# Gate and up projections of two feed-forward layers by one level of Strassen, with moving weights and token-major results

## The chip, the core and the metric

The kernel runs on one core of one Trainium2 chip, as one program. The metric is the device time of one execution in microseconds, taken as the median of several runs. In the profile PE is TensorE (its weight loads, which overlap its matmuls, stand as PEld), DVE is VectorE, ACT is ScalarE, POOL is GpSimd and SP is SyncE, whose queue starts the loads of the weights.

## The reference

Two layers, 512 tokens, 1024 features, 2816 hidden features, all in float32. Layer 0 mixes tokens by a gated linear recurrence (RG-LRU), layer 1 by stick-breaking attention with 16 heads. Each mixer is followed by a feed-forward part, which is what the change touches:

```python
for layer in range(DEPTH):
    h = _rmsnorm(x, norm_mix_g[layer])
    x = x + mixer(h)                        # RG-LRU or attention
    h = _rmsnorm(x, norm_ffn_g[layer])
    g = h @ w_gate                          # 512x1024 @ 1024x2816
    u = h @ w_up                            # 512x1024 @ 1024x2816
    x = x + (silu(g) * u) @ w_down          # 512x2816 @ 2816x1024
return _rmsnorm(x, final_g)
```

`_rmsnorm` multiplies each token by 1/sqrt(mean of its squares + 1e-6) and each feature by g.

## The kernel before

**Layout.** The activations stand transposed: eight tiles `x[0..7]` of 128 features (partitions) x 512 tokens. A product is made in PSUM banks of 128 x 512, with a 128 x 128 block of weights as the stationary operand and activations as the moving one. Each operand is split into a rounded high part (type fp32r) and a remainder, and a product is three matmuls (`mm3`, L163 to L167): high x high, high x low, low x high.

**Weights.** They come in chunks of 128 x 1024 elements (512 KB), in the order of one list made by `plan` (L81). `chunk` (L151) hands out the next one, and on the way starts loads (four chunks ahead, on SP's queue, into four buffers `raw`) and splits (two ahead, three buffers each of `wh` and `wl`): ScalarE casts raw to wh (L136), and VectorE or GpSimd takes wl = raw - wh (L137; `wl_engine` gives odd chunks to GpSimd and even ones to VectorE, but for a few given by hand).

**The norm.** As soon as a tile x[k] has its residual added, `norm_in` (L215) makes its two operands uh and ul (ScalarE L219, VectorE L220) without the token's factor, and `norm_sq` (L229) squares it on ScalarE (L235) and adds the square into `acc` (L237; GpSimd, the last tile on VectorE). `norm_rs1` (L251) sums acc over partitions by four one-column matmuls (L255), and `rsqrt` makes the token factors `rsT`, one token a partition. `norm_rs2` (L259) spreads them over all partitions by four matmuls (L263), into `rsB`.

**A feed-forward layer** (`ffn`, L455) has 22 tiles of 128 hidden features. Each is a gate product and an up product of 24 matmuls (8 feature tiles x 3) and an evacuation (L460 to L468): both are multiplied by rsB on VectorE, the gate goes through Silu on ScalarE, and the product of both is split into `fh` and `fl`. norm_rs1 stands behind the first gate product, norm_rs2 behind the first up product. All 22 pairs stay in SBUF. Then the eight output tiles follow, each 22 x 3 matmuls over three chunks (`DOWN_SPLIT`), and a residual addition (L490). In layer 1 the last output tile is made in two halves of 256 tokens (L493 to L501), so that `finish` (L266), which makes the final norm and writes the output for one half of the tokens, works on the first half while TensorE makes the second.

The last part of each mixer is its output projection: tile by tile 24 matmuls, a residual addition (L450 in layer 0, L731 in layer 1) and `norm_in`. The order on each engine's queue comes from a scheduler that follows data and priorities; the splits of weights have a raised priority (L143). In the attention the order on PE, ACT, DVE and POOL is written out by hand.

Of the kernel before, what the change touches and what calls it, by code (L numbers as in the profile page):

```python
# [16 lines left out]
P = 128  # L17
S = 512
# [11 lines left out]
NSLOT = 73  # L30
WARM = 9
DOWN_SPLIT = ((0, 8), (8, 15), (15, 22))
# [9 lines left out]

class Kern:
    def __init__(self, ctx, tc, a, out):
        self.ctx, self.tc, self.nc, self.a, self.out = ctx, tc, tc.nc, a, out
        mk = lambda name, bufs, **kw: ctx.enter_context(tc.tile_pool(name=name, bufs=bufs, **kw))
        self.const = mk("const", 1)
        self.wp = mk("wp", 1)
        self.tp = mk("tp", 1)
        self.ar = mk("ar", 1)  # L50
        self.free = deque(range(NSLOT))
        self.slot = {}
        pp = mk("pp", 1, space=bass.MemoryType.PSUM)
        self.bank = [pp.tile([P, S], F32, name=f"bank{i}") for i in range(8)]
        self.bi = 0
        self.tn = 0
        self.wl_dve = False
        self.wl_on = {**dict.fromkeys((*range(5, 12), 14), self.nc.gpsimd),
                      **dict.fromkeys((2, 3, 4, 12, 13, 15, 16, 17, 18, 19), self.nc.vector)}
# [6 lines left out]
    def new(self, name, dt=F32, shape=None):  # L66
        i = self.free.popleft()
        self.tn += 1
        t = self.ar.tile(shape or [P, S], dt, tag=f"s{i}", bufs=1, name=f"{name}_{self.tn}")
        self.slot[id(t)] = (i, t)  # L70
        return t

    def rel(self, *ts_):
        for t in ts_:
            self.free.append(self.slot.pop(id(t))[0])
# [5 lines left out]
    def plan(self):  # L81
# [13 lines left out]
        def ffn(l):  # L95
            r = []
            for f in range(NF):
                r += [a["w_gu"][l, f, 0], a["w_gu"][l, f, 1]]
            for m in range(8):
                r += [a["w_dn"][l, m, :, lo * P:hi * P] for lo, hi in DOWN_SPLIT]  # L100
            return r

        full += ffn(0)
        full += [a["w_v"][c] for c in range(8)]
# [5 lines left out]
        self.wq = {}  # L110
        self.loaded = self.split = self.used = 0
# [4 lines left out]

    def raw_tile(self, i):
        t = self.wp.tile([P, 1024], F32, tag="raw", bufs=4, name=f"raw{i}")
        self.raw[i] = (t, self.chunks[i].shape[-1])
# [3 lines left out]
    def load_one(self):  # L123
        src = self.chunks[self.loaded]
        t = self.raw_tile(self.loaded)
        self.nc.sync.dma_start(t[:, :src.shape[-1]], src)

    def split_tiles(self, i):
        wh = self.wp.tile([P, 1024], F32R, tag="wh", bufs=3, name=f"wh{i}")
        wl = self.wp.tile([P, 1024], F32R, tag="wl", bufs=3, name=f"wl{i}")  # L130
        self.wq[i] = (wh, wl)
        self.split += 1
# [6 lines left out]
    def split_one(self):  # L139
        i = self.split  # L140
        raw, n = self.raw.pop(i)
        wh, wl = self.split_tiles(i)
        with self.tc.high_priority(self.PRI):  # L143
            self.split_piece(i, raw, wh, wl, slice(0, n))

    def wl_engine(self, i):
        if i in self.wl_on:
            return self.wl_on[i]
        return self.nc.gpsimd if i % 2 and not self.wl_dve else self.nc.vector

    def chunk(self, ahead=None):  # L151
        i = self.used
        self.used += 1
        n = len(self.chunks)
        while self.loaded < min(n, i + self.AHEAD_LOAD):
            self.load_one()
        while self.split < min(n, i + (ahead or self.AHEAD_SPLIT)):
            self.split_one()
            while self.loaded < min(n, self.split + self.AHEAD_LOAD - self.AHEAD_SPLIT + 1):
# [18 lines left out]
    def setup(self):  # L178
# [3 lines left out]
        self.u = [None] * KT  # L182
        self.par = c.tile([P, NPAR], F32, name="par")
# [40 lines left out]

    def free_u(self):
# [13 lines left out]
    def rsqrt(self, ss, lo, hi):  # L239
# [8 lines left out]
        for t in range(lo, hi):  # L248
            self.dgi = nc.vector.tensor_scalar(self.dg[:, ts(t)], self.ident, self.rsT[:, t:t + 1], None, ALU.mult)

    def norm_rs1(self):  # L251
# [4 lines left out]
        self.dg = self.tmp()  # L256
# [41 lines left out]
    def rglru(self):  # L298
        nc, tc = self.nc, self.tc
        with ExitStack() as cx:  # L300
            rp = cx.enter_context(tc.tile_pool(name="rg", bufs=1))
# [21 lines left out]
            def evac_x(m, ps):  # L323
                xc[m], ah[m], al[m] = self.new("xc"), self.new("ah", F32R), self.new("al", F32R)
# [63 lines left out]
            def tile_x2():  # L388
                p = (self.ps(), self.ps())
                raws = [self.raw.pop(i)[0] for i in range(2)]  # L390
# [56 lines left out]
            for m in range(KT):  # L447
# [3 lines left out]
                self.norm_in(m, "g_ffn0")  # L451
# [3 lines left out]
    def ffn(self, l, gnext):  # L455
        nc, tc = self.nc, self.tc
        if True:
            ah, al = [None] * NF, [None] * NF

            def evac(f, pg, pu):  # L460
                tg, tu = self.tmp(), self.tmp()
                nc.vector.tensor_tensor(tg, pg, self.rsB, ALU.mult)  # L462
                self.last = nc.scalar.activation(tg, tg, AF.Silu)
                nc.vector.tensor_tensor(tu, pu, self.rsB, ALU.mult)  # L464
                nc.vector.tensor_tensor(tu, tu, tg, ALU.mult)
                ah[f], al[f] = self.new("fh", F32R), self.new("fl", F32R)
                nc.scalar.copy(ah[f], tu)  # L467
                nc.gpsimd.tensor_tensor(al[f], tu, ah[f].bitcast(F32), ALU.subtract)  # L468

            for f in range(NF):  # L470
                pg = self.ps()
                self.mm_tile(pg, self.u)
                if f == 0:
                    self.norm_rs1()
                pu = self.ps()
                self.mm_tile(pu, self.u)
                if f == 0:
                    self.norm_rs2()
                evac(f, pg, pu)
            self.free_u()  # L480
# [3 lines left out]
            for m in range(KT if gnext else KT - 1):  # L484
                p = self.ps()
                for lo, hi in DOWN_SPLIT:
                    wh, wl = self.chunk()
                    for k in range(lo, hi):
                        self.mm3(p, wh[:, ts(k - lo)], wl[:, ts(k - lo)], ah[k], al[k], k == 0, k == NF - 1)
                nc.vector.tensor_tensor(self.x[m], self.x[m], p, ALU.add)  # L490
                self.norm_in(m, gnext)
            if gnext is None:
                ws = [self.chunk() for _ in DOWN_SPLIT]  # L493
                for j in range(2):
                    cs = ts(j, HS)
                    p = self.ps()
                    for (lo, hi), (wh, wl) in zip(DOWN_SPLIT, ws):
                        for k in range(lo, hi):
                            self.mm3(p[:, :HS], wh[:, ts(k - lo)], wl[:, ts(k - lo)], ah[k][:, cs], al[k][:, cs],
                                     k == 0, k == NF - 1)  # L500
                    self.finish(j, p)  # L501
            for t in ah + al:
                self.rel(t)

    def attention(self):
# [4 lines left out]
        with ExitStack() as cx:  # L510
            ap_ = cx.enter_context(tc.tile_pool(name="att", bufs=1))
            vs = [[None] * 4 for _ in range(NT)]
# [24 lines left out]
            for half in range(2):  # L537
# [12 lines left out]
                for t in range(NT):  # L550
                    r = self.rsT[:, t:t + 1]
                    pvv = pv[t].rearrange("p (h d) -> p h d", d=64)
                    for j in range(2):
                        v = vs[t][2 * half + j] = self.new("vs", F32R, [P, 4, P])
# [149 lines left out]
            with tc.manual_schedule(engines={E.PE, E.Activation, E.DVE, E.Pool}):  # L704
# [10 lines left out]
                def osplit(p):  # L715
                    oh, ol = ou[p] = self.new("oh", F32R), self.new("ol", F32R)
# [13 lines left out]
                def out_evac(m):  # L730
                    nc.vector.tensor_tensor(self.x[m], self.x[m], outs.pop(m)[0], ALU.add)  # L731
                    self.norm_in(m, "g_ffn1")
# [74 lines left out]
def layout(inp):  # L807
# [7 lines left out]
    def cols(v):  # L815
# [11 lines left out]
    gu = np.stack([np.stack([stat(g("ffn_w_gate")[l]), stat(g("ffn_w_up")[l])], axis=1) for l in range(2)])  # L827
    dn = np.stack([stat(g("ffn_w_down")[l]) for l in range(2)])
# [9 lines left out]
        "w_gu": c(gu),  # L838
        "w_dn": c(dn),
# [17 lines left out]
```

## Time and profile before

| | |
|---|---|
| time, median of 3 runs | 1214.06 us (1213.08 to 1214.74) |
| time of the profiled execution | 1214.85 us |
| span of the profiled execution | 1213.1 us, 13743 instructions |
| mean granted clock of TensorE | 0.995 |
| data from HBM | 102.81 MB, 86 GB/s over the span |

The span runs from the first to the last instruction of the profiled execution, and the time holds what lies around it too. Of a stretch (A:B), a row gives its length, then for PE, PEld, DVE, ACT and POOL the busy time with the number of instructions, then the mean granted clock (1.00 is full), the share of the time that the DMA engines were busy, and GB/s. A row of a timeline has the start in us, the duration, the engine, the line, the operation, and output <- input. A row of a group has the line, the engine, the operation, the number of instructions, the busy time, the mean duration in ns, and the idle time of the engine ahead of them with what ended it; where a source line is looked at, the three figures are the least, the median and the greatest duration in ns. Buffer numbers are left out of the names.

### The profile page before, as it was taken

The numbers are of one execution on the slowest core, as the hardware profiler recorded it, in microseconds if no ns is written. First come the engines' busy times: TensorE is split into PE (matmuls) and PEld (weight loads), VectorE is DVE, ScalarE is ACT, GpSimd is POOL, SyncE is SP. The second block draws the span as 40 slices with busy tenths as digits, with TensorE's granted clock in tenths as the row PEclk, the third lists the DMA queues.
The fourth block names the chain that finished last, engine by engine and source line by source line (L and its number), as shares of the span: only waits on it lengthen the run. The fifth ranks groups of instructions, "written<-read, shape, count | busy, mean of one in ns | idle before, by whom it ended". The sixth has DMA issues, their size and how long they took to land.

```text
span 1213.1 us, 13743 instructions
## 1 busy us (share of the span) xinstructions
PE 1165.5 (96%) x5347; PEld 955.4 (79%) x5347; DVE 581.4 (48%) x790; ACT 521.6 (43%) x751; POOL 457.8 (38%) x283
## 2 busy tenths in 40 slices
PE   9999999999999999999978888799999999999996
PEld 6877788888888888888857766578888888888886
DVE  7878652333223222223799999975322233321112
ACT  6687443323323222224677777654323232332221
POOL 2442343333333223321266665533333333332332
PEclk9999999999999999999999999999999999999998
DMA  7222322232323333332111111122222223233321
GB/s 241 79 82 92 117 88 89 102 104 87 104 87 100 96 96 96 100 105 87 53 35 35 38 50 36 35 70 95 97 90 101 91 101 105 85 96 96 96 64 70
DMA packets 31313, 105.80 MB, mean 87 GB/s; under 512 B 3600, under 2 KB 4624, under 8 KB 31248
## 3 DMA queue, kind: packets, MB, share of 16 engines
q1 hardware_dynamic: 30960, 104.40, 26.8%
q8 instruction: 42, 0.69, 0.2%
q10 hardware_dynamic: 288, 0.52, 0.1%
q14 instruction: 23, 0.19, 0.0%
HBM read 102.81 MB, written 2.10 MB: 86 GB/s over the span
## 4 chain that ended last, share of the span: by engine, by line
PE 74%; DVE 14%; issue 3%; ACT 1%; POOL 0%; DVEq 0%; ACTq 0%; POOLq 0%
PE bank L165 24%; PE bank L167 24%; PE bank L166 24%; DVE sph L636 2%; DVE t L635 2%; DVE wl L137 2%; DVE r L642 1%; DVE awh L678 1%; DVE awl L683 1%; DVE o L701 1%; DVE ql L590 1%; DVE ks L597 1%; DVE t L576 1%; PE bank L662 1%; DVE t L641 0%
## 5 line engine op out<-in xcount | busy, mean ns | idle before, releaser
L136 ACT CAST wh<-raw 128x1024 fp32r<-128x1024 f32 (+2 forms) x202 | 203.4, 1010 | 531.6 <-PE bank L166 279.0
L165 PE MATMUL bank<-uh,wh 128*128 128x512 f32 x960 | 376.8, 393 | 9.0 <-DVE t L576 8.1
L167 PE MATMUL bank<-uh,wl 128*128 128x512 f32 x960 | 374.0, 390 | 1.3 <-DVE wl L137 1.3
L166 PE MATMUL bank<-ul,wh 128*128 128x512 f32 x960 | 373.8, 389 | 0.3 <-DVE ul L220 0.3
L137 POOL TENSOR_TENSOR wl<-raw,wh 128x1024 fp32r<-128x1024 f32 (+2 forms) x95 | 219.6, 2312 | 361.5 <-ACT wh L136 361.5
L165 PEld LDWEIGHTS bank<-uh,wh 128*128 128x128 f32 x960 | 180.6, 188 | 47.8 <-issue 9.5
L167 PEld LDWEIGHTS bank<-uh,wl 128*128 128x128 f32 x960 | 180.2, 188 | 40.5 <-DVE wl L137 2.5
L166 PEld LDWEIGHTS bank<-ul,wh 128*128 128x128 f32 x960 | 180.4, 188 | 37.2 <-DVE ul L220 0.6
L137 DVE TENSOR_TENSOR wl<-raw,wh 128x1024 fp32r<-128x1024 f32 (+2 forms) x107 | 136.1, 1274 | 137.2 <-ACT wh L136 136.2
L468 POOL TENSOR_TENSOR fl<-t,fh 128x512 fp32r<-128x512 f32 x44 | 67.2, 1528 | 198.4 <-ACT fh L467 198.4
L165 PE MATMUL bank<-fh,wh 128*128 128x512 f32 (+1 forms) x374 | 141.1, 377 | 0.0
L166 PE MATMUL bank<-fl,wh 128*128 128x512 f32 (+1 forms) x374 | 140.8, 376 | 0.0
L167 PE MATMUL bank<-fh,wl 128*128 128x512 f32 (+1 forms) x374 | 140.8, 376 | 0.0
L464 DVE TENSOR_TENSOR t<-bank,rsB 128x512 f32<-128x512 f32 x44 | 30.4, 691 | 199.4 <-PE bank L167 199.4
L462 DVE TENSOR_TENSOR t<-bank,rsB 128x512 f32<-128x512 f32 x44 | 30.4, 691 | 116.7 <-PE bank L167 116.7
L637 POOL TENSOR_TENSOR spl<-t,sph 128x512 fp32r<-128x512 f32 (+1 forms) x48 | 58.8, 1230 | 65.4 <-DVE sph L636 51.6
L166 PEld LDWEIGHTS bank<-fl,wh 128*128 128x128 f32 x374 | 70.4, 188 | 13.0
L167 PEld LDWEIGHTS bank<-fh,wl 128*128 128x128 f32 x374 | 70.4, 188 | 12.9
L165 PEld LDWEIGHTS bank<-fh,wh 128*128 128x128 f32 x374 | 70.4, 188 | 12.7
L237 POOL TENSOR_TENSOR acc<-acc,t 128x512 f32<-128x512 f32 x24 | 38.5, 1606 | 52.1 <-ACT t L235 43.4
L683 POOL TENSOR_TENSOR awl<-t,awh 128x512 fp32r<-128x512 f32 x28 | 40.0, 1427 | 41.2 <-DVE awh L678 41.2
L490 DVE TENSOR_TENSOR x<-x,bank 128x512 f32<-128x512 f32 x15 | 10.3, 687 | 74.7 <-PE bank L167 74.7
(166 smaller groups left out, 1456.4 us busy)
## 6 DMA issues: line engine op xcount, KB each, us to landing
raw<-w_gu SPq DMA_DIRECT2D x88, 512.0 KB, 3.5
raw<-w_dn SPq DMA_DIRECT2D x32, 448.0 KB, 3.3
raw<-w_dn SPq DMA_DIRECT2D x16, 512.0 KB, 3.5
raw<-w_qk SPq DMA_DIRECT2D x16, 512.0 KB, 3.4
raw<-w_in SPq DMA_DIRECT2D x14, 512.0 KB, 3.7
raw<-w_ao SPq DMA_DIRECT2D x8, 512.0 KB, 3.5
raw<-w_v SPq DMA_DIRECT2D x8, 512.0 KB, 3.4
raw<-w_bo SPq DMA_DIRECT2D x8, 512.0 KB, 3.4
```

What stands on the lines that cost most here:

```text
L136: self.nc.scalar.copy(wh[:, c], raw[:, c])
L137: self.wl_engine(i).tensor_tensor(wl[:, c], raw[:, c], wh[:, c].bitcast(F32), ALU.subtract)
L165: mm(out, lhsT=wh, rhs=xh, start=first, stop=False)
L166: mm(out, lhsT=wh, rhs=xl, start=False, stop=False)
L167: mm(out, lhsT=wl, rhs=xh, start=False, stop=last)
L237: self.acci = eng.tensor_tensor(self.acc, self.acc, sq, ALU.add)
L462: nc.vector.tensor_tensor(tg, pg, self.rsB, ALU.mult)
L464: nc.vector.tensor_tensor(tu, pu, self.rsB, ALU.mult)
L468: nc.gpsimd.tensor_tensor(al[f], tu, ah[f].bitcast(F32), ALU.subtract)
L635: nc.vector.scalar_tensor_tensor(sp[:, :w], z, 0.0, e[:, :w], ALU.max, ALU.add)
L637: nc.gpsimd.tensor_tensor(sl[:, :w], sp[:, :w], sh[:, :w].bitcast(F32), ALU.subtract)
L683: eng.tensor_tensor(wl[:, :w], ts_[i][:, :w], hd["wh"][i][:, :w].bitcast(F32), ALU.subtract)
```

## The change

Gate and up of a layer are one matrix product: A (512 tokens x 1024 features) times B (1024 features x gate and up). It is now made by one level of Strassen's method in Winograd's form. A is cut into tokens 0 to 255 and 256 to 511, and into features 0 to 511 and 512 to 1023 (A11, A12, A21, A22). B is cut into quarters b0 (gate, first features), b1 (up, first), b2 (gate, second) and b3 (up, second). In place of eight products of quarters there are seven, in this order:

- 1: A11 with b0
- 5: (A21 + A22) with b1 - b0
- 6: (A21 + A22 - A11) with b3 - b1 + b0
- 3: (A12 - A21 - A22 + A11) with b3
- 7: (A11 - A21) with b3 - b1
- 2: A12 with b2
- 4: A22 with b2 - (b3 - b1 + b0)

The sums of results give gate and up of all 512 tokens.

**Units.** The hidden features are taken in five units of 512 and one of 256 (`Unit`, `FB`, `NU`). A product of a full unit takes two chunks of weights and 4 feature tiles x 2 token tiles x 3 = 24 matmuls, 12 a chunk. The activations are now the stationary operand (128 x 128) and the weights the moving one (512 columns, 256 in the last unit), and the result has tokens on its partitions. So the token factor is a scalar of a partition (rsT), and norm_rs2 is gone in the feed-forward part. Results are gathered in SBUF tiles r1, u2 and b5, two each.

**Operands.** `ffn_in` takes the place of `norm_in` behind the mixers. For tiles 0 to 3 it makes the operand of product 1 alone. For tiles 4 to 7 it scales x[m] and x[m - 4] on ScalarE, makes four sums of 256 tokens on VectorE (L331 and L346), and splits three tiles (ScalarE casts, VectorE remainders). The sums of the weights are made by VectorE too: `Piece.source` (L76) has four for each chunk position, eight a full unit, of 128 x 1024, in place or in two buffers `tt`. All splits of these weights have their remainder on VectorE, those of the down weights on GpSimd.

**The rings.** In the feed-forward part the rings of wh and wl have four buffers, splits run three chunks ahead and loads eight, the latter partly into buffers of the layer's own pool (b1, b3). The arena of 73 slots becomes 43 and a pool of 30 that belongs to the mixers.

**Down, unit by unit.** While unit u is made, the results of unit u - 1 are transposed back by TensorE (`turn`: eight 128 x 128 transposes into two banks, L627; ScalarE copies the high part hh, L630; VectorE subtracts the remainder hl, L631), two of its four tiles behind product 1 and two behind product 5. Four `down_pair` follow between the products, each 24 matmuls (L640 to L642) into the same two banks, and an addition into x (L645). The last unit's turn stands at the end, and behind it eight tiles of six matmuls; in layer 1 the last tile again in two halves with `finish`.

```diff
+    def source(self):
...
+        if q == 7:
+            sub(b(1), b(3), b(1))
...
+        if q == 5:
...
+            sub(b("t"), b(1), b(0))
+        elif q == 6:
+            sub(b("t"), b(3), b("t"))
+        else:
+            sub(b("t"), b(2), b("t"))
+        return b("t")
...
+            def turn(fs, banks):
+                for f, b in zip(fs, banks):
+                    for t in range(NT):
+                        nc.tensor.transpose(b[:, ts(t)], (u2 + b5)[t][:, ts(f)], self.ident)
...
+                    nc.scalar.copy(h, b)
+                    nc.vector.tensor_tensor(lw, b, h.bitcast(F32), ALU.subtract)
...
+                product(1, un, A, 0)
+                for j in range(2):
+                    nc.scalar.copy(r1[j][:, :w], A[j][:, :w])
+                if u == 0:
+                    self.bi = 6
+                    self.norm_rs1(False)
+                else:
+                    turn((0, 1), tb)
+                product(5, un, B, 0)
+                if u > 0:
+                    turn((2, 3), tb)
+                for j in range(2):
+                    nc.scalar.copy(b5[j][:, :w], B[j][:, :w])
+                if u > 0:
+                    down_pair(0)
+                product(6, un, A, 0, False)
...
+                if 0 < u < NU:
+                    down_pair(1)
+                product(3, un, B, 0, False)
...
+            turn((0, 1), (A[0], A[1]))
...
+                    if m == KT - 1 and split7:
+                        for j in range(2):
+                            down(w, i, 2, p7[j], first=False, cs=hs[j])
+                            self.bi = 4 + 2 * j
+                            self.finish(j, p7[j])
+                        continue
```

In the feed-forward part PE's order is written out by hand; the other engines' follows from the scheduler. Three places of the order show what moved.

VectorE at the start of layer 0's feed-forward part. x_7 and x_8 are the last two tiles of x, acc the sum of squares, wl the remainder of a weight chunk, and ul that of an operand. Before:

```order
L450 TENSOR_TENSOR x_7_84<-x_7_84,bank_75 128x512
L220 SCALAR_TENSOR_TENSOR ul_1349<-x_7_84,par,uh_1348 128x512
L450 TENSOR_TENSOR x_8_85<-x_8_85,bank_76 128x512
L137 TENSOR_TENSOR wl_1440<-raw_1321,wh_1439 128x1024
L220 SCALAR_TENSOR_TENSOR ul_1387<-x_8_85,par,uh_1386 128x512
L237 TENSOR_TENSOR acc<-acc,t_1390 128x512
```

Now, from the fourth row behind the addition into x_8 (three sums of 256 tokens stand between): t are operand sums, ol their remainders, tt the sums of weights.

```order
L331 TENSOR_TENSOR ol_1454<-t_1436,oh_1453 128x512
L76 TENSOR_TENSOR tt_1485<-b_178_1473,raw_1244 128x1024
L331 TENSOR_TENSOR t_1438<-t_1436,t_1437 128x256
L76 TENSOR_TENSOR tt_1503<-b_179_1475,raw_1300 128x1024
L234 TENSOR_TENSOR wl_1488<-tt_1485,wh_1487 128x1024
L331 TENSOR_TENSOR ol_1446<-t_1437,oh_1445 128x512
L234 TENSOR_TENSOR wl_1506<-tt_1503,wh_1505 128x1024
L76 TENSOR_TENSOR tt_1485<-b_180_1477,tt_1485 128x1024
L331 TENSOR_TENSOR ol_1450<-t_1438,oh_1449 128x512
L76 TENSOR_TENSOR tt_1503<-b_181_1479,tt_1503 128x1024
L234 TENSOR_TENSOR wl_1535<-tt_1485,wh_1534 128x1024
L371 TENSOR_TENSOR acc<-acc,t_1457 128x512
```

Two rows stood between the last residual addition and that into acc before; now fourteen do, seven of them 1024 wide.

TensorE at the same place. bank_71 is the second bank of product 1, bank_72 the first of product 5. Before (uh and ul are the operands that norm_in made; the rows ahead of L255 end the first gate product):

```order
L165 MATMUL bank_77<-uh_1386,wh_1355 128x512
L166 MATMUL bank_77<-ul_1387,wh_1355 128x512
L167 MATMUL bank_77<-uh_1386,wl_1356 128x512
L255 MATMUL bank_70<-ones,acc 128x1 x4
L165 MATMUL bank_71<-uh_1122,wh_1394 128x512
L166 MATMUL bank_71<-ul_1123,wh_1394 128x512
```

Now:

```order
L621 MATMUL bank_71<-wl_1482,a_130_1234 128x512
L622 MATMUL bank_71<-wh_1481,a_130_1234 128x512
L389 MATMUL bank_76<-ones,acc 128x1 x4
L620 MATMUL bank_72<-wh_1487,oh_1281 128x512
L621 MATMUL bank_72<-wl_1488,oh_1281 128x512
L622 MATMUL bank_72<-wh_1487,ol_1282 128x512
```

The four matmuls that read acc stand 24 matmuls into the layer both times; behind them stood the rest of the layer, and so it does now.

ScalarE at a second turn (unit 1 of layer 0, tiles hh_82 in banks 76 and 77), beside the steady gate and up of before. Before:

```order
L136 CAST wh_1624<-raw_1518 128x1024
L463 ACTIVATE t_1614<-t_1614 128x512
L136 CAST wh_1654<-raw_1558 128x1024
L467 CAST fh_1620<-t_1615 128x512
L136 CAST wh_1694<-raw_1588 128x1024
L463 ACTIVATE t_1684<-t_1684 128x512
```

Now:

```order
L630 CAST hh_80_2677<-bank_76 128x512
L630 CAST hh_80_2685<-bank_77 128x512
L233 CAST wh_2743<-tt_2653 128x1024
L233 CAST wh_2773<-raw_2615 128x1024
L630 CAST hh_82_2728<-bank_76 128x512
L630 CAST hh_82_2736<-bank_77 128x512
L669 COPY b_1471<-bank_72 128x512
L669 COPY b_1472<-bank_73 128x512
```

Two weight casts (L233) stand between the copies of the first turn and those of the second, and the copies of the second stand ahead of the copies of product 5's banks.

357 lines of the change are left out of this document (276 added, 81 removed).

## The prediction

> **What bounds the kernel now.** First the page: its head, the busy shares and the shares of the chain that ended last.
>
> ```profile
> span 1213.1 us, 13743 instructions
> PE 1165.5 (96%) x5347; PEld 955.4 (79%) x5347; DVE 581.4 (48%) x790; ACT 521.6 (43%) x751; POOL 457.8 (38%) x283
> ...
> PE 74%; DVE 14%; issue 3%; ACT 1%; POOL 0%; DVEq 0%; ACTq 0%; POOLq 0%
> ```
>
> TensorE (PE) is busy 96% of the span. A share over a whole kernel hides stages, so next come the busy times by stretches, chosen inside the feed-forward layers (two of layer 0, two of layer 1).
>
> ```profile
> 172.50:345.00 172.50, 172.50 (x771) 143.05 (x770) 52.35 (x73) 55.17 (x68) 61.29 (x31) 1.00 0.29 95
> 345.00:527.50 182.50, 182.50 (x807) 151.12 (x806) 47.52 (x50) 51.23 (x62) 61.38 (x31) 1.00 0.32 96
> 843.50:1021.00 177.50, 177.50 (x793) 147.19 (x792) 54.04 (x74) 57.07 (x70) 63.02 (x33) 1.00 0.29 95
> 1021.00:1199.00 178.00, 178.00 (x844) 149.74 (x843) 38.35 (x54) 45.47 (x56) 59.68 (x34) 1.00 0.27 80
> ```
>
> PE is busy in every microsecond at full granted clock (1.00); VectorE (DVE, fifth figure) is under a third busy. In these layers the time is the number of matmuls times their spacing, which the timeline gives: every third start of a 512-wide stream, and starts nine apart of a 256-wide one. The last three rows mark where the layers begin and end.
>
> ```profile
> 1165.13 0.39 PE L165 MATMUL bank<-fh,wh 128*128 128x512 f32 x1
> 1165.81 0.39 PE L165 MATMUL bank<-fh,wh 128*128 128x512 f32 x1
> ...
> 1198.32 0.28 PE L165 MATMUL bank<-fh,wh 128*128 128x256 f32 x1
> 1199.40 0.28 PE L165 MATMUL bank<-fh,wh 128*128 128x256 f32 x1
> ...
> 167.40 0.69 DVE L450 TENSOR_TENSOR x<-x,bank 128x512 f32<-128x512 f32 x1 [1.55 <-PE bank L167]
> 528.13 0.39 PE L165 MATMUL bank<-wh,uh 128*128 128x512 f32 x1
> 838.20 0.39 PE L165 MATMUL bank<-uh,wh 128*128 128x512 f32 x1
> ```
>
> 0.68/3 = 0.227 us for 512 columns, 1.08/9 = 0.12 us for 256. Layer 0 begins some 0.2 us before its last residual addition (167.2) and ends at 528.1: 361 us, of which 1584 matmuls at 0.227 are 359. Call the start of a layer T0. Nothing waits there, so every wait that the change brings in is new.
>
> **Products saved.** Gate and up are 1056 matmuls a layer now. After: 5 units of 168 at 512 columns and one of 168 at 256. 840 x 0.227 + 168 x 0.12 = 190.4 + 20.2 = 210.6 against 1056 x 0.227 = 239.4: **28.8 us less a layer**. The down products stay 528 x 0.227. The second half of the norm (four 128-wide f32 matmuls, 179.84 - 179.03 = 0.8 us below) goes: -0.8.
>
> ```profile
> 179.03 1.06 PE L263 MATMUL bank<-t,ones 128*128 128x128 f32 x8
> 179.84 0.47 PE L165 MATMUL bank<-uh,wh 128*128 128x512 f32 x1
> ```
>
> **The wait at the start of a layer.** In the changed PE order the four matmuls of the norm statistic stand behind product 1 and ahead of product 5, and read acc. PE keeps order, so all products queue behind them. Before, acc was ready early (last addition at 841.11, PE reached its statistic 5.4 us after 838.2). Now, in VectorE's own queue, the last addition into acc stands behind the operand sums of tile 7, four weight sums and three weight splits. Their prices:
>
> ```profile
> 841.11 0.69 DVE L237 TENSOR_TENSOR acc<-acc,t 128x512 f32<-128x512 f32 x1
> ...
> L137 DVE TENSOR_TENSOR wl<-raw,wh x107: 417/1219/3370, 5.3 to 1180.4; 128x1024 fp32r<-128x1024 f32 x87, 128x896 fp32r<-128x896 f32 x16, 128x256 fp32r<-128x256 f32 x4
> ...
> L465 DVE TENSOR_TENSOR t<-t,t 128x512 f32<-128x512 f32 x44 | 30.5, 692 | 4.8 <-ACT wh L136 0.5
> L641 DVE TENSOR_TENSOR t<-t 128x256 f32<-128x256 f32 x16 | 6.6, 415 | 0.0
> L219 ACT ACTIVATE uh<-x,par 128x512 fp32r<-128x512 f32 x32 | 23.0, 723 | 5.9 <-DMA x<-xT 3.0 <-DVE x L731 2.7
> L237 POOL TENSOR_TENSOR acc<-acc,t 128x512 f32<-128x512 f32 x24 | 38.5, 1606 | 52.1 <-ACT t L235 43.4 <-DVE wl L137 8.7
> ```
>
> From T0: residual addition 0.69 (with 0.2 of handoff), two ScalarE scalings 1.45, then on VectorE four half-tile sums at 0.42, three remainders at 0.69, seven 1024-wide operations at 1.22, the addition 0.69: 0.9 + 1.45 + 1.7 + 2.1 + 8.5 + 0.7 = 15.3 us. Product 1 covers 24 x 0.227 = 5.4, so PE waits **9.9 us at least**. VectorE also comes late to T0: each of tiles 4 to 7 now costs it 0.69 + 1.5 + 1.7 + 2.1 = 6.0 us while PE makes a tile in 5.4, so 3 x 0.6 = 1.8 us of lag without disturbance. The disturbance is GpSimd, which adds the squares into acc (1.6 us a tile):
>
> ```profile
> 162.91 2.39 POOL L137 TENSOR_TENSOR wl<-raw,wh 128x1024 fp32r<-128x1024 f32 x1 [2.44 <-ACT wh L136]
> 163.49 2.37 DVE L220 SCALAR_TENSOR_TENSOR ul<-x,par,uh 128x512 fp32r<-128x512 f32 x1 [0.84 <-ACT uh L219]
> ```
>
> A 0.75 us operation of VectorE took 2.37 and ended 0.56 after GpSimd's: it stood still meanwhile. With 1.6 more a tile the lag is 3 x 2.2 = 6.6. I take 4.1, about the middle, since some of GpSimd's additions will fall into VectorE's own waits: **14.0 us a layer** (11.7 to 16.5). The Trainium skill (SBUF — State Buffer, Who interferes with whom) says that a VectorE instruction with two SBUF inputs and a GpSimd instruction that reads SBUF exclude one another for the whole instruction; the two rows agree. By that rule the lag would be near its upper end and the sum 5 us higher over both layers, and it speaks against moving splits and sums onto VectorE.
>
> After such an idle stretch the granted clock is lower. Two stretches at the kernel's end, PE nearly idle in the first:
>
> ```profile
> 1201.70:1204.80 3.10, 0.97 (x9) 0.80 (x7) 1.46 (x8) 0.68 (x2) 0.00 (x0) 0.95 0.12 47
> 1204.80:1206.10 1.30, 1.22 (x4) 0.93 (x4) 0.16 (x1) 0.02 (x1) 0.00 (x0) 0.50 0.00 0
> ```
>
> Half clock after some 3 us of little work. How long it takes to return isn't shown; I take **2 us a layer** lost (0 to 3.5). By the Trainium skill (TensorE: Matmul & The Clock Gate, Part 1) full clock returns after one window of 3.4 us of work, which would lose 1.7 us; no row here shows the return.
>
> What the wait buys: VectorE has run ahead, so the rest of unit 0 is not late.
>
> **The turns.** Each of the 5 later units has two turns of eight 128-wide f32 transposes. One transpose lies between 0.12 - (0.227 - 0.12)/2 = 0.066 (the spacing rows, drawn on to 128 columns) and 0.20 (0.81/4, L263, same type and shape, two records a matmul). Neither is nearer; I take 0.12. The first turn costs eight: 1.0 us (0.5 to 1.6); its evacuation hides behind product 5 (5.4 us). The second one's doesn't: the down pair behind it writes the bank just transposed into, and waits until ScalarE has copied and VectorE subtracted it. On ScalarE a weight cast stands ahead of those copies, and its buffer comes free only at product 5's end.
>
> ```profile
> L136 ACT CAST wh<-raw 128x1024 fp32r<-128x1024 f32 (+2 forms) x202 | 203.4, 1010 | 531.6 <-PE bank L166 279.0 <-issue 210.6 <-PE bank L167 22.0
> ...
> L382 ACT CAST ah<-bank 128x512 fp32r<-128x512 f32 x8 | 4.5, 586 | 1.9 <-DVE bank L381 1.9
> L383 DVE TENSOR_TENSOR al<-bank,ah 128x512 fp32r<-128x512 f32 x8 | 5.1, 681 | 0.7 <-ACT ah L382 0.7
> ```
>
> 0.25 handoff + 1.05 + 0.59 + 0.68 + 0.1 = **2.65 us** from product 5's end to the down pair, transposes included (2.0 if the cast weren't first, 3.6 if VectorE holds a 1.22 us split too). Five units: 5 x (1.0 + 2.65) = 18.2. The last turn has no product behind it: eight transposes and 1.4 until its second remainder: 2.4. Together **20.6 us a layer** (14.5 to 29).
>
> The other added work is covered. Per full unit VectorE has 22 operations of 1.22 and 22 of 0.69, 42 us, plus up to 4 x 2.39 behind GpSimd, against a unit of 62 us; a split is due three chunks (8 us) before its use. Loads: 12 of 512 KB a unit, 100 GB/s, as now (95). ScalarE: 25 us of 62.
>
> **The end.** Before, the first half's finish hid behind 66 matmuls of the second (66 x 0.12 = 7.9). Now six stand there (0.7 us).
>
> ```profile
> 1201.76 0.42 DVE L271 TENSOR_TENSOR x<-x,bank 128x256 f32<-128x256 f32 x1 [2.47 <-PE bank L167]
> ...
> 1206.55 2.44 DVE L295 SCALAR_TENSOR_TENSOR y<-x,par,bank 128x256 f32<-128x256 f32 x6 [1.59 <-issue]
> ```
>
> From a half's addition to the end of its outputs: 4.8 + 2.4 = 7.2 us, and the second half's addition stands behind those outputs on VectorE: 7.2 - 0.7 = 6.5 exposed, less 1.6 that PE now spends on the first finish. Six additions into acc at 1.6 against tiles of 6 x 0.227 = 1.4 are late by up to 2. I take **5.5** (4 to 7.5).
>
> **Sum.** A layer: -28.8 - 0.8 + 14.0 + 2.0 + 20.6 = +7.0. Two layers and the end: +19.5. The profiled execution took 1214.85 us (span 1213.1 and 1.75 around it), 0.8 above the runs' median of 1214.06. 1214.06 + 19.5 = **1233.6**. All low bounds together: 2 x (-29.6 + 11.7 + 14.5) + 4 = -3, so 1211; all high ones 2 x (-29.6 + 16.5 + 3.5 + 29) + 7.5 = +46, so 1260.
>
> The Trainium skill (TensorE: Matmul & The Clock Gate, Part 4) gives about 275 ns for a PE transpose inside one kernel; by it the turns that aren't hidden would bring the sum 14 us higher, to 1247.
>
> **Rivals.** (1) *VectorE does the new f32 sums at twice the rate, and the change wins.* At half of VectorE's prices the start's chain is 0.6 + 1.45 + 6.5 = 8.5 us, with no lag, so the wait is 3.1 and the clock stays up; the turns lose 0.4 each; the end costs 4.3. A layer: -29.6 + 3.1 + 18.5 = -8.0; in all -11.7, so 1202. Between that and the forecast, zero lies at about two thirds of the rows' prices. Against it: the median of 1219 ns over 107 operations of the same kind. The Trainium skill (VectorE: DVE Perf Modes, Side-by-side) gives f32 tensor_tensor one element a cycle; 1024 elements in 1219 ns agree. (2) *VectorE sets the pace inside the units.* 42 us of 62, and up to 52 with GpSimd's exclusion, in a queue where evacuations wait for PE: if a weight sum waits for a load whose buffer GpSimd frees late, each unit loses 2 to 4 us: 10 x 3 = +30, so 1264. For it: the raw buffers are still four, for loads on a longer path; against it: each split is due 8 us ahead. (3) *The clock drops at every second turn:* 2 us x 10 = +20, so 1254. For it is the 0.50 row; against it, only 1.7 us of those 2.65 are idle. (4) *The prices all lie near their low bounds:* 1211 from the sum of them, no change or slightly faster.
>
> **Chances.** Forecast (1214 to 1250) 0.70; rival 1 0.05; rival 2 0.09; rival 3 0.06; rival 4 0.10, half of it faster. A measurement of this kernel can tell 0.2% (2.4 us). Faster 0.05 + 0.05 = 0.10, same 0.05, slower 0.85. The range 1214 to 1254 leaves out rivals 1 and 2, most of rival 4 on its low side, and the last few us that all high bounds at once would give.
>
> **What would show it.** In the changed profile PE's idle time should name the acc addition at both layer starts (about 14 us each), the remainder of the second turn (1.7 us, ten times) and, at the end, the second half's addition. L620 to L622 should number 2016 in all, spaced 0.227 at 512 columns. It is wrong if the starts wait under 6 us, if the down pairs follow their turns at once, or if PE's largest idle names a weight split inside the units.

## The result and the profile after

The changed kernel takes 1240.95 us (median of 4 runs, 1240.10 to 1241.45), the kernel before 1214.40 (4 runs, 1213.08 to 1215.42). The ratio is 1.0219, with a 95% interval of 1.0201 to 1.0236: 26.5 us slower, where 19.5 had been forecast (1233.6, range 1214 to 1254).

The head of the page of the changed kernel, then two stretches: the start of layer 0's feed-forward part and its middle.

```profile
span 1239.7 us, 14201 instructions
PE 1149.1 (93%) x5363; PEld 946.8 (76%) x5363; DVE 878.8 (71%) x1105; ACT 640.5 (52%) x919; POOL 349.4 (28%) x218
```

```profile
165.00:200.00 35.00, 21.85 (x87) 17.82 (x86) 26.88 (x37) 18.30 (x26) 1.77 (x1) 0.76 0.36 121
200.00:500.00 300.00, 290.02 (x1359) 241.61 (x1358) 194.32 (x210) 128.54 (x158) 44.90 (x18) 1.00 0.28 94
```

TensorE has less to do, and idles. Over 300 us of the middle it lacks 10 us, but of the first 35 us it lacks 13, at a granted clock of 0.76. VectorE went from 48% to 71% of the span. What TensorE waited for stands in the view of waits: its line, whose result it waited for, the sum in us, the number of waits, and the longest.

```profile
PE bank L389 <- DVE acc L371: 17.9, 2, 13.2
PE bank L640 <- DVE hl L631: 15.1, 10, 1.5
...
PE bank L627 <- DVE b L697: 4.9, 4, 1.6
PE bank L620 <- DVE x L970: 4.3, 1, 4.3
```

Two entries carry the forecast: the statistic of the norm waits for the addition into acc, twice, and the down pair waits for the remainder hl, ten times. The places, from TensorE's timeline:

```profile
165.31 0.39 PE L620 MATMUL bank<-wh,a 128*128 128x512 f32 x1
...
184.06 1.86 PE L389 MATMUL bank<-ones,acc 128*128 128x1 f32 x8 [13.15 <-DVE acc L371]
185.79 0.77 PE L620 MATMUL bank<-wh,oh 128*128 128x512 f32 x1
186.36 0.63 PE L621 MATMUL bank<-wl,oh 128*128 128x512 f32 x1
...
191.01 0.39 PE L620 MATMUL bank<-wh,oh 128*128 128x512 f32 x1
...
228.45 0.33 PE L627 MATMUL bank<-ident,b 128*128 128x128 f32 x1 [1.55 <-DVE b L697]
...
234.55 0.38 PE L627 MATMUL bank<-ident,u 128*128 128x128 f32 x2
...
237.10 0.50 PE L640 MATMUL bank<-hh,wh 128*128 128x512 f32 x1 [1.52 <-DVE hl L631]
237.43 0.39 PE L641 MATMUL bank<-hl,wh 128*128 128x512 f32 x1
...
535.85 0.39 PE L267 MATMUL bank<-wh,uh 128*128 128x512 f32 x1
849.46 0.39 PE L269 MATMUL bank<-oh,wl 128*128 128x512 f32 x1
854.16 0.77 PE L620 MATMUL bank<-wh,a 128*128 128x512 f32 x1 [4.31 <-DVE x L970]
...
867.33 1.86 PE L389 MATMUL bank<-ones,acc 128*128 128x1 f32 x8 [4.74 <-DVE acc L371]
...
1206.27 0.38 PE L627 MATMUL bank<-ident,u 128*128 128x128 f32 x2
```

The first row is the start of layer 0's feed-forward part, 535.85 its end, 849.69 (849.46 and one spacing) the point at which layer 1's would begin, and 1206.27 the last turn. So the 26.6 us between the two spans fall on these stages:

| stage | before | after | difference | forecast |
|---|---|---|---|---|
| to the start of layer 0's feed-forward part | 167.2 | 165.3 | -1.9 | 0 |
| feed-forward part of layer 0 | 360.9 | 370.5 | +9.6 | +7.0 |
| attention, to layer 1's feed-forward part | 310.1 | 313.8 | +3.8 | 0 |
| feed-forward part of layer 1 and the end | 374.9 | 390.0 | +15.1 | +12.5 |

The -1.9 stands ahead of the new instructions: 0.9 of it arises in the first 10 us, the rest at waits between 108 and 126 us, and in the profiles of the runs below that stage ends anywhere between 165.4 and 167.8 us (last section). So stages are compared below, beside the medians.

VectorE at the start of layer 0: the last residual addition, the first sum of weights and the addition into acc.

```profile
170.07 0.68 DVE L585 TENSOR_TENSOR x<-x,bank 128x512 f32<-128x512 f32 x1
...
173.83 1.22 DVE L76 TENSOR_TENSOR tt<-b,raw 128x1024 f32<-128x1024 f32 x1
...
183.31 0.69 DVE L371 TENSOR_TENSOR acc<-acc,t 128x512 f32<-128x512 f32 x1
```

The residual addition stands 4.8 us behind the start at 165.31, and from it to the addition into acc are 13.2 us.

### The profile page after: what moved, and what is told of

It reads as the page before. It is cut to its first block, busy times and chain, and to the rows that moved or that the text cites. A ratio compares the mean times of both kernels' runs of the same rounds, so it can differ in the third digit from the quotient of the medians.

```text
span 1239.7 us, 14201 instructions
## 1 busy us (share of the span) xinstructions
PE 1149.1 (93%) x5363; PEld 946.8 (76%) x5363; DVE 878.8 (71%) x1105; ACT 640.5 (52%) x919; POOL 349.4 (28%) x218
## 5 line engine op out<-in xcount | busy, mean ns | idle before, releaser
L234 POOL TENSOR_TENSOR wl<-raw,wh 128x1024 fp32r<-128x1024 f32 (+1 forms) x74 | 180.8, 2443 | 694.6 <-ACT wh L233 692.3
L233 ACT CAST wh<-raw 128x1024 fp32r<-128x1024 f32 (+1 forms) x154 | 156.0, 1017 | 198.6 <-PE bank L622 93.8
L620 PE MATMUL bank<-wh,oh 128*128 128x512 f32 (+1 forms) x576 | 217.0, 377 | 0.0
L621 PE MATMUL bank<-wl,oh 128*128 128x512 f32 (+1 forms) x576 | 215.7, 375 | 0.0
L622 PE MATMUL bank<-wh,ol 128*128 128x512 f32 (+1 forms) x576 | 215.6, 374 | 0.0
L640 PE MATMUL bank<-hh,wh 128*128 128x512 f32 (+1 forms) x358 | 139.9, 391 | 15.6 <-DVE hl L631 15.1
L645 DVE TENSOR_TENSOR x<-x,bank 128x512 f32<-128x512 f32 x87 | 59.7, 686 | 114.5 <-PE bank L642 113.4
L641 PE MATMUL bank<-hl,wh 128*128 128x512 f32 (+1 forms) x358 | 138.6, 387 | 0.4 <-DVE hl L631 0.4
L642 PE MATMUL bank<-hh,wl 128*128 128x512 f32 (+1 forms) x358 | 138.4, 387 | 0.0
L622 PEld LDWEIGHTS bank<-wh,ol 128*128 128x128 f32 x576 | 109.6, 190 | 19.3
L620 PEld LDWEIGHTS bank<-wh,oh 128*128 128x128 f32 x576 | 109.8, 191 | 18.8
L233 ACT CAST wh<-tt 128x1024 fp32r<-128x1024 f32 x66 | 69.5, 1053 | 93.2 <-PE bank L622 46.0
L233 ACT CAST wh<-b 128x1024 fp32r<-128x1024 f32 x44 | 46.4, 1053 | 127.6 <-PE bank L622 44.8
L267 PE MATMUL bank<-uh,wh 128*128 128x512 f32 x256 | 104.6, 409 | 6.8 <-DVE t L814 4.3
L268 PE MATMUL bank<-ul,wh 128*128 128x512 f32 x256 | 101.6, 397 | 0.3 <-DVE ul L323 0.3
L269 PE MATMUL bank<-uh,wl 128*128 128x512 f32 x256 | 101.3, 396 | 0.0
L640 PEld LDWEIGHTS bank<-hh,wh 128*128 128x128 f32 x358 | 67.5, 189 | 31.5 <-DVE hl L631 17.5
```

What stands on the lines that cost most here:

```text
L233: self.nc.scalar.copy(wh[:, c], raw[:, c])
L234: self.wl_engine(i).tensor_tensor(wl[:, c], raw[:, c], wh[:, c].bitcast(F32), ALU.subtract)
L267: mm(out, lhsT=wh, rhs=xh, start=first, stop=False)
L268: mm(out, lhsT=wh, rhs=xl, start=False, stop=False)
L269: mm(out, lhsT=wl, rhs=xh, start=False, stop=last)
L620: mm(out[j][:, :w], lhsT=oh[:, ts(j)], rhs=wh[:, ws], start=st, stop=False, skip_group_check=True)
```

## The experiments

**The statistic moved.** norm_rs1 of unit 0 stands behind product 7, ahead of its first use.

```diff
-                if u == 0:
-                    self.bi = 6
-                    self.norm_rs1(False)
-                else:
+                if u > 0:
                     turn((0, 1), tb)
...
+                if u == 0:
+                    self.bi = 6
+                    self.norm_rs1(False)
                 product(2, un, D, 0)
```

> Theory (VectorE's queue sets the start, and TensorE's read of acc makes the whole queue's end the barrier): with the statistic behind product 7, product 5 waits only for its own first split, which ended at 177.7 us in layer 0 and 860.9 in layer 1 of the changed kernel, instead of the addition into acc. Layer 0 then gains 185.8 - 177.7 = 8.1 us, layer 1 869.05 - 862.5 = 6.5 and the 2.3 us of half clock behind it; less 0.3 a layer for the statistic at full clock: 16 us in all, 1225 us, with 7 us of idle time still in front of product 5 of layer 0. Rival (the operands and splits of products 5 and 6 are as late as acc): under 4 us gained, 1237 or more, and the idle time moves to products 5 and 6 in full.

It took 1229.71 us (ratio to the kernel before 1.0132, 1.0109 to 1.0155), 11 less than the changed kernel. Its runs lie apart (two at 1227.3, two near 1232.2), and the profile is of one of the first two; why the others took 5 us longer isn't known. In it layer 0's feed-forward part took 363.3 us (7.2 less), and layer 1's with the end shrank by 8.7. Its view of waits has no acc any more:

```profile
PE bank L640 <- DVE hl L631: 15.0, 10, 1.5
...
PE bank L620 <- ACT wh L233: 5.3, 1, 5.3
PE bank L620 <- DVE x L970: 4.3, 1, 4.3
```

In acc's place product 5 of layer 0 waits 5.3 us for the cast of its first weight sum, where 7 had been expected. Of the 16 us the stages of this profile gave 15.9. The theory holds: the statistic made the whole of VectorE's queue a barrier, and behind it a shorter one shows.

**All four tiles turned at once.** The second pair is transposed behind product 1 too, into banks D, which product 2 needs only later.

```diff
                     turn((0, 1), tb)
+                    turn((2, 3), D)
                 product(5, un, B, 0)
-                if u > 0:
-                    turn((2, 3), tb)
```

> Theory (the second turn's gap is the reuse of the bank just transposed into, with the copies and remainders in between): with all sixteen transposes behind product 1, the second pair into two banks that are free then, the chain of copies hides behind product 5 and only the transposes stay, 0.79 us a turn. Each unit gains 2.55 - 0.79 = 1.76 us, ten units 17.6: 1223 us. Rival (VectorE's queue makes the remainders late wherever they stand): the down pair waits as long as now, behind product 5; gain under 4 us, 1237 or more.

It took 1218.79 us (ratio 1.0038, 1.0024 to 1.0053), 22 us less than the changed kernel. The rows are a turn of unit 2 of layer 0, its first and last, and product 5 behind it:

```profile
288.73 0.38 PE L627 MATMUL bank<-ident,u 128*128 128x128 f32 x2
...
290.25 0.38 PE L627 MATMUL bank<-ident,b 128*128 128x128 f32 x2
290.39 0.48 PE L620 MATMUL bank<-wh,oh 128*128 128x512 f32 x1
```

Sixteen transposes take 1.66 us, and nothing waits here; the entry for hl is gone from the waits. (In unit 5 of each layer a wait of 0.9 us for L697 stays.) The gap was the reuse of the bank, and VectorE has the time. The gain is 4 us over the forecast: the wait for L697 in unit 1 (1.55, both layers) went as well, and with each gap the first matmuls behind it, some 0.1 us longer.

**The remainders' engines in the attention.** Stages show 3.8 us lost where no instruction was added before its last part. Near its end, VectorE and GpSimd in the changed kernel:

```profile
804.07 3.30 DVE L921 TENSOR_TENSOR awl<-t,awh 128x384 fp32r<-128x384 f32 x2
```

```profile
803.83 2.52 POOL L234 TENSOR_TENSOR wl<-raw,wh 128x1024 fp32r<-128x1024 f32 x1
```

```diff
-        return self.nc.gpsimd if i % 2 and not self.wl_dve else self.nc.vector
+        return self.nc.gpsimd if (i + (i >= self.after[0])) % 2 and not self.wl_dve else self.nc.vector
```

> The number of chunks of a feed-forward layer is odd in the changed kernel, so that behind layer 0 the chunks whose remainder GpSimd makes and those that VectorE makes have changed places; here they change back. Theory (this costs the attention its 3.8 us: a 1024-wide remainder on GpSimd, 2.5 us, stands over two VectorE remainders that take 3.30 us in place of 1.15): the stretch from the end of layer 0 to the start of layer 1 shrinks from 318.3 by 3 to 4 us, 1237.5 us. Rival (the new operand work for layer 1's feed-forward part, in the same VectorE queue, costs it): the stretch stays within 1 us, 1241.

```profile
806.00 1.15 DVE L921 TENSOR_TENSOR awl<-t,awh 128x384 fp32r<-128x384 f32 x2
```

The two remainders take 1.15 us again, and the stretch, which includes layer 1's first wait, shrank from 318.3 to 315.6. The median was 1240.21 (ratio 1.0217, 1.0202 to 1.0232), only 0.7 lower; in the profile, 1.8 us more went into the first stage. So the swap cost 2.7 of the 3.8 us. Where the other 1.1 went was not tried.

**The end.** `finish` yields behind its addition, its statistic and its broadcast, and the two halves go through these steps together.

```diff
-                            self.bi = 4 + 2 * j
-                            self.finish(j, p7[j])
+                        for _ in zip_longest(*(self.finish(j, p7[j]) for j in range(2))):
+                            pass
```

> Theory (the second half's addition stands behind the first half's outputs on VectorE): with both additions first and both statistics ahead of all outputs, the second half's outputs follow the first half's at once. The last output begins at about 1228.5 instead of 1233.0 in the changed kernel's profile: 4 us gained (3 to 5), 1237. Rival (the first half's own chain from the addition into acc, and the outputs, set the end): under 1.5 us gained, 1239.5 or more.

The changed kernel's VectorE (the two halves' additions and outputs), then this run's:

```profile
1218.63 0.42 DVE L405 TENSOR_TENSOR x<-x,bank 128x256 f32<-128x256 f32 x1
...
1225.37 2.44 DVE L429 SCALAR_TENSOR_TENSOR y<-x,par,bank 128x256 f32<-128x256 f32 x6 [1.52 <-ACT rsB L417]
1227.73 0.42 DVE L405 TENSOR_TENSOR x<-x,bank 128x256 f32<-128x256 f32 x1
...
1232.98 2.44 DVE L429 SCALAR_TENSOR_TENSOR y<-x,par,bank 128x256 f32<-128x256 f32 x6 [1.52 <-ACT rsB L417]
```

```profile
1220.13 0.42 DVE L406 TENSOR_TENSOR x<-x,bank 128x256 f32<-128x256 f32 x1
1220.85 0.42 DVE L406 TENSOR_TENSOR x<-x,bank 128x256 f32<-128x256 f32 x1 [0.29 <-PE bank L646]
...
1228.29 4.79 DVE L433 SCALAR_TENSOR_TENSOR y<-x,par,bank 128x256 f32<-128x256 f32 x12 [0.87 <-ACT rsB L420]
```

From the first half's addition to the end of the last output it was 1235.4 - 1218.6 = 16.8 us, and is 1233.1 - 1220.1 = 13.0: 3.8 less, as the theory has it. The median, 1238.86 (ratio 1.0196, 1.0181 to 1.0212), is 2.1 lower, with 1.6 us more in the first stage of the profile.

**Idle time filled.** Matmuls whose result nobody reads stand ahead of the statistic, 54 in layer 0 and 18 in layer 1.

```diff
+                    for _ in range(FILL[l]):
+                        mm(tb[1], lhsT=self.held[0][:, ts(0)], rhs=self.held[0], start=True, stop=True)
                     self.bi = 6
                     self.norm_rs1(False)
```

> 54 matmuls in layer 0 and 18 in layer 1, whose result nobody reads, fill the idle time between product 1 and the statistic. Theory (half clock follows idle time of TensorE): product 5 starts at 0.227 us spacing in both layers, and 2.6 + 2.3 us are gained; the clock loss at product 1 of layer 1 stays: 1236 us. Rival (half clock comes with the switch of weights or with the four-pass statistic, not with idle time): spacing 0.43 for 4.5 us as now, 1241 us.

It took 1234.00 us (ratio 1.0159, 1.0144 to 1.0174), 7 less. The first row is 40 of the filler's matmuls:

```profile
173.03 9.23 PE L663 MATMUL bank<-a 128*128 128x512 f32 x40
...
185.27 0.95 PE L390 MATMUL bank<-ones,acc 128*128 128x1 f32 x8
186.08 0.48 PE L621 MATMUL bank<-wh,oh 128*128 128x512 f32 x1
186.40 0.39 PE L622 MATMUL bank<-wl,oh 128*128 128x512 f32 x1
```

The half clock is gone, so it follows idle time. From product 5's start to the first turn are 38.2 us instead of 40.6 (2.4 gained), and the statistic itself takes 0.8 instead of 1.7. The comparison isn't clean: the scheduler moved the addition into acc ahead of two sums and a split on VectorE, and the filler was then 2.4 us too long.

**Four edits together**: the statistic, the four turns, the engines and the end.

> The statistic behind product 7, all four transposed tiles behind product 1, the remainders' engines as before in the attention, and both halves at the end together. Theory (the four waits are separate places on TensorE's path): the gains that the stages of the single runs showed add up, 15.9 + 22 + 3.5 + 3.6 = 45 us, 1196 us, which is below the kernel before. Rival (they share VectorE's queue, so that one wait takes another's place): 10 us less, 1206.

It took 1196.62 us (ratio 0.9860, 0.9844 to 0.9877), 44 under the changed kernel and 18 under the kernel before. The waits were separate places, and the gains add up.

**Product 2 second in unit 0.** Besides, the list of chunks has that order in unit 0.

```diff
+                else:
+                    product(2, un, D, 0)
                 product(5, un, B, 0)
...
-        return [Piece(k, q, c) for q in (1, 5, 6, 3, 7, 2, 4) for c in range(k.np)]
+        qs = (1, 5, 6, 3, 7, 2, 4) if u else (1, 2, 5, 6, 3, 7, 4)
+        return [Piece(k, q, c) for q in qs for c in range(k.np)]
```

> As the run with all four edits, and in unit 0 product 2, which needs no sum of weights, stands second. Theory (what is left at the start of layer 0 is product 5's wait for VectorE's weight sum and split, 5.3 us): product 2 fills it, and with it goes the half clock behind it: 7 us in layer 0, under 1 in layer 1, where product 5 hardly waits: 7 us under the run with four edits. Rival (VectorE has no spare time there, and the sums for products 6 and 3 come late instead): under 2 us gained.

It took 1203.78 us (ratio 0.9916, 0.9901 to 0.9930), 7 more, not less: the rival. In the profiles 2.4 of it stands in the first stage, 1.1 in layer 0's feed-forward part and 4.5 in layer 1's with the end. TensorE's waits in this run:

```profile
PE bank L632 <- DVE b L704: 3.8, 4, 1.7
PE bank L626 <- DVE wl L236: 3.7, 3, 1.6
...
PE bank L625 <- DVE b L687: 3.1, 2, 2.3
```

Product 5's wait is gone, but splits come late three times (3.7 us in all), an addition in layer 1 by 2.3, and the last evacuation of unit 0 again ahead of the turn (1.7), the last two with half clock behind them. VectorE had no slack there; its backlog only moved. In this run the statistic also stands 24 matmuls closer to the turn, which takes part in the last of these; how much, it doesn't show.

**Additions into acc on VectorE**, in `ffn_in` of the changed kernel:

```diff
-        self.norm_sq(m)
+        self.norm_sq(m, nc.vector)
```

> The changed kernel with all additions into acc ahead of a feed-forward layer on VectorE. Theory (VectorE stands still while GpSimd adds: the 256-wide sum that took 1.52 us takes 0.42): VectorE has 0.6 more and 1.1 less a tile, the last residual addition comes about 0.5 us a tile earlier, and each layer's start gains 1.5 us: 1238 us. Rival (the 1.52 us have another cause): each tile costs 0.6 more, 3 to 4 us over both layers, 1244.5.

It took 1238.28 us (ratio 1.0200, 1.0184 to 1.0215), 2.7 less, as the theory has it. By stages, layer 0's feed-forward part gained 2.7 and the attention, with layer 1's first wait, 2.1; the first stage took 1.9 more. One of the sums for a tile's operands:

```profile
167.59 0.42 DVE L331 TENSOR_TENSOR t<-t,t 128x256 f32<-128x256 f32 x1
```

In the changed kernel the same sum took 1.52 us while GpSimd added from 166.72 to 168.49:

```profile
167.25 1.52 DVE L331 TENSOR_TENSOR t<-t,t 128x256 f32<-128x256 f32 x1
```

```profile
166.72 1.77 POOL L371 TENSOR_TENSOR acc<-acc,t 128x512 f32<-128x512 f32 x1 [4.82 <-ACT t L369]
```

The Trainium skill (SBUF — State Buffer, Who interferes with whom) has a VectorE instruction with two SBUF inputs contend with a GpSimd instruction that reads SBUF; this and the remainders above (3.30 against 1.15) agree.

**The same added to the four edits**, ahead of both feed-forward layers and behind the last.

> As the run with four edits (1196.6 us), with the additions into acc on VectorE ahead of both feed-forward layers and behind the last one. Theory (GpSimd's additions hold VectorE up, so that operands and sums of weights come earlier without them, whoever waits for acc): 2.3 us in layer 0 and 2 us ahead of layer 1, as the run with that edit alone showed, and 1 us at the end where six additions on GpSimd are late by 1.7: 1191.5 us. Rival (with the statistic late, acc is on no path any more): within 1 us of 1196.6.

It took 1194.94 us (ratio 0.9839, 0.9825 to 0.9852), 1.7 less than without: between the two. Layer 0's feed-forward part gained 2.2 (351.9 to 349.7), the attention's stretch 1.4, and the end behind the last turn 1.5, but layer 1's part ahead of that lost 1.1. That makes 4.0 us, nearer to the theory's 5 than the medians show; the first stage of this profile is 2.1 us longer than that of the run with four edits.

**And the two idle stretches filled**, before product 5 of layer 0 and product 1 of layer 1.

> As the run before in this group, with matmuls whose result nobody reads in TensorE's two idle stretches: 14 in front of product 5 of layer 0 and 9 in front of product 1 of layer 1. Theory (half clock follows the idle time): no stretch of 0.43 us spacing is left behind these places, 1.3 to 2.6 us a layer: 3.5 us under the run with acc moved, 1188 us. Rival (the filler only changes places with idle time): the same time as that run, or up to 1 us above it.

It took 1193.31 us (1191.27 to 1195.22; ratio 0.9831, 0.9818 to 0.9845). The starting stretch of the run before, then of this one:

```profile
165.00:200.00 35.00, 30.84 (x127) 24.47 (x126) 31.29 (x39) 21.30 (x29) 0.00 (x0) 0.95 0.50 169
```

```profile
165.00:200.00 35.00, 32.72 (x147) 26.47 (x146) 31.79 (x39) 20.19 (x27) 0.00 (x0) 1.00 0.56 180
```

The clock is full, 1.00 against 0.95, but the time is only 1.6 us lower, where 3.5 had been expected, and the two kernels' runs overlap (1194.05 to 1195.82 without the filler). The stages behind the first also gave 1.6. In layer 1 the first turn now waits 1.9 us for the last evacuation of unit 0, which it didn't in the run before. This kernel has the lowest median, 21 us under the kernel before.

## Why the prediction was right

**Saved products.** L620 to L622 are 2016 matmuls, and the spacing at 512 columns is 0.227 us. With the term of -29.6 us a layer, the parts below add up to the measured stages within 1 us.

**The start: the mechanism right, a wait in layer 1 not seen.** The chain was put at 15.3 us from T0 with 4.1 of lag, so acc at T0 + 19.4; it was ready at 184.0, T0 + 18.7. The last residual addition came a little later than forecast (T0 + 4.8 for 4.3), and the chain from it on was shorter (13.9 us for 15.1). The wait in layer 0 was 13.3 us (14.0 forecast), and with the statistic at half clock (1.7) product 5 began 15.0 us late. In layer 1 half of the wait came earlier: product 1's own bank, in which the attention's last tile is made, had not been read by the last residual addition (4.3), a wait that the prediction didn't see, and the statistic then waited 4.7 instead of 13. With the half clock the two came to 13.9. The barrier was the one named, since moving the statistic took 15.9 us away in the profile.

**The clock: undersized.** Two us a layer were forecast. From 185.79 the spacing was 0.43 until 190.8 us, which loses 2.5, and layer 1 has two such stretches, 854.2 to 859.9 (2.8 lost) and 869.05 to 873.5 (2.2), because it has two waits. The Trainium skill (TensorE: Matmul & The Clock Gate, Part 1) has full clock after one busy window of 3.4 us, in a window that runs freely; counted from the first matmul of the statistic, it came after 6.7 us in layer 0 and 6.2 at the same place in layer 1, so between one and two windows. Wait and clock together were put at 16.0 us a layer; less the 0.8 that the statistic takes at full clock, they came to 16.7 and 15.3. In layer 1 that is luck: shorter waits made up for the second half-clock stretch.

**The turns: the sum near, by luck in its parts.** 20.6 us a layer were forecast, 20.9 came up to the first matmul behind each turn, and some 22.4 with the slower ones that follow it: over the usual spacing, second turns cost 2.55 (2.65 forecast), first turns 0.79 in units 2 to 4 (1.0), but 2.56 in unit 1 and 1.9 in unit 5, where the transposes waited for the last evacuation of the unit ahead (L697). The prediction looked only at the evacuation behind the first turn, not at the one ahead of it. A transpose takes 0.10 us by spacing, less than the 0.12 taken, and the last turn cost 1.3 where 2.4 had been taken; these offset it. The second turn's chain was as forecast. In unit 1, on ScalarE and then on VectorE:

```profile
234.79 1.04 ACT L233 CAST wh<-raw 128x1024 fp32r<-128x1024 f32 x1 [1.71 <-PE bank L622]
235.74 1.06 ACT L630 CAST hh<-bank 128x512 fp32r<-128x512 f32 x2
```

```profile
236.35 1.29 DVE L631 TENSOR_TENSOR hl<-bank,hh 128x512 fp32r<-128x512 f32 x2 [2.02 <-ACT hh L630]
```

The weight cast, released by product 5's end, stands ahead of the copies and is 0.95 of the 2.55 us. What moving that cast alone would have given was not tried.

**The end.** +5.5 forecast; as 12.8 us lie between layer 0's last turn and its end, layer 1's tail behind that is 1239.74 - 1206.27 - 12.78 = 20.7 us against 1213.1 - 838.2 - 360.9 = 14.0 before: +6.7. The second half's addition did stand behind the first half's outputs.

**What was left out.** The attention was costed at nothing, without a word. The count of chunks of a feed-forward layer went from 68 to 99, which is odd, and swapped the engines of the remainders behind it: 2.7 us of the 3.8 that the stage lost. The forecast is 7 us low: 3.8 from this, some 3.5 from the turns with the matmuls behind them and 1.2 from the end, less 1.9 in the first stage; the start with its clock came out even over the two layers.

**The rivals.** VectorE's price is 1.22 us for a 1024-wide sum, so rival 1 (twice the rate) falls. Inside the units TensorE waits for no weight split, so rival 2 falls; it came up only when a run moved work into the start. The matmul behind a second turn takes 0.50 us and the next ones 0.39, so the clock holds and rival 3 falls. The start and the second turns came near the values taken, not near their low bounds, so rival 4 falls.

## What to carry to other kernels

Fewer products are only worth what is left when TensorE, which keeps order, meets no result of a slower queue: here 59 us saved became 26 lost, a difference of 86. Moving two barriers (a statistic that nobody needed yet, and a bank reused at once) won back 38 of it in the single runs, and with two smaller repairs gave a kernel 1.4% faster than before. Most of what that kernel still loses stands in the turns (11.7 us a layer over the usual spacing) and in the waits and half clock at the starts of the layers (8.8 and 6.7). When an instruction on the critical engine reads a result, ask how much stands ahead of that result on its own queue, and whether the reader could stand later. A change of a loop's count can swap engines far behind it, wherever they are dealt out by the parity of a running index.

## What was not expected of the hardware

The record of a transpose is 0.27 us long (0.272 median), but sixteen in a row start 0.104 us apart (1.66 / 16). The Trainium skill (TensorE: Matmul & The Clock Gate, Part 4) gives about 275 ns for a bf16 one inside a kernel; that agrees with the record's length, not with what a transpose costs in a row. At half clock the statistic's eight matmuls took 1.73 us until the next one, at full clock 0.81.

The same wait is not always followed by half clock. In layer 0's mixer TensorE waits 2.2 us for L566 at 108 us. In the changed kernel the clock stays up behind it; in the run with the attention's engines changed back it falls at 112.4, and some 1.6 us are lost:

```profile
110.71 0.47 PE L267 MATMUL bank<-uh,wh 128*128 128x512 f32 x1 [2.18 <-DVE gt L566]
...
112.63 0.40 PE L269 MATMUL bank<-uh,wl 128*128 128x512 f32 x1
```

```profile
110.91 0.47 PE L267 MATMUL bank<-uh,wh 128*128 128x512 f32 x1 [2.16 <-DVE gt L566]
...
112.45 0.63 PE L267 MATMUL bank<-uh,wh 128*128 128x512 f32 x1
```

The edit touches nothing at that place, so a wait of this length costs either itself alone or itself and 1.6 us. The granted clock in the other profiles says the same: of the changed kernel and the runs above, the four without half clock in this stage end it at 165.3 to 165.7 us, and the six with half clock behind this wait at 167.0 to 167.8. (In the run with acc on VectorE the half clock stands at 8.5 us, and the stage ends at 167.2.) That is as much as a small edit is worth, and the reason for comparing stages.
